# Rotary embedding on one core: the first batch is stored by two DMAs (2 and 30 KB rows) instead of three (2, 14 and 16 KB rows)

## The chip, the cores and the metric

One core of a Trainium2 chip. The metric is the time of one execution on the device in microseconds (us), the median of several runs.

## What is computed

```python
def reference(x, cos, sin):          # x: (8, 2048, 8, 64), cos and sin: (2048, 32), float32
    x1 = x[..., : x.shape[-1] // 2]
    x2 = x[..., x.shape[-1] // 2 :]
    cos = cos[None, :, None, :]
    sin = sin[None, :, None, :]
    out1 = x1 * cos - x2 * sin
    out2 = x1 * sin + x2 * cos
    return np.concatenate([out1, out2], axis=-1)
```

x is 32 MB and is read once; the output has the same size and is written once.

## The kernel before

**Tiles.** Each of the 8 batches is one tile `xt` of 128 partitions by 8192 float32 elements: partition q holds 16 consecutive positions of the sequence (`R = 16`), each of 8 heads by 64 elements, `HD = 512` elements or 2 KB. A row of a tile is thus 32 KB, and a batch is 4 MB. `UNIT` is 4 HD. Five buffers (`NBUF`) hold the tiles; the result is written over x in place, and the tile is stored from there.

**Loads.** All loads are issued from SP's queue (line 67). Batch 0 is loaded in three DMAs (8, 8 and 16 KB rows), every other batch in one DMA with 32 KB rows. The loads of batches 0 to 4 are issued at the start. The load of batch b + 5 is issued after the work of batch b, and waits until batch b's store has freed the buffer.

**Compute.** A batch is worked on in pieces, `pieces(b)`: batch 0 in pieces of 2, 2, 4, 4 and 4 HD, the last one in 4, 4, 4, 2 and 2, the others in four of 4. For a piece of kind A, GpSimd (POOL) multiplies by sin and by -sin (two instructions, line 122), VectorE (DVE) multiplies by cos (line 129), and then adds the two products into `xt` (line 136). Five pieces are of kind B or C, in which TensorE adds the two products with identity matrices and ScalarE (ACT) copies the sum into `xt` (lines 143 to 145 and 160 to 165); in kind C the sin product is DVE's as well (line 148). These are the first pieces of batches 1 to 5.

**Stores.** A batch is stored in the shares that `shares(b)` lists. A share is issued as soon as the pieces that cover it are done (line 74), from ACT's queue, for the last batch from SP's. A store on ACT's queue is issued in ACT's program order, between its copies.

**Order.** The order of the instructions is that of the program (`keep`). The loads and the last batch's stores are in one DMA queue (q1 in the profile), the other stores and the load of sin in another (q10). Both are worked on by the same 16 DMA engines; a DMA over 128 partitions is split into 128 rows, 8 on each engine.

Of the kernel before, what the change touches and what calls it, by code (L numbers as in the profile page):

```python
# [10 lines left out]
def kernel(  # L11
# [15 lines left out]
    HD = H * D  # L27
    R = S // P
    ROW = R * HD
    UNIT = 4 * HD  # L30
# [145 lines left out]

    def shares(b):
        if b == 0:
            return [HD, 7 * HD, 2 * UNIT]
        if b == last:  # L180
            return [2 * UNIT, UNIT, UNIT]
        return [ROW]

    for b in range(B):
        done = 0
        outs = list(spans(shares(b)))
        for lo, n in spans(pieces(b)):
            rotate(b, lo, n)
            done = lo + n
            while outs and sum(outs[0]) <= done:  # L190
                store(b, *outs.pop(0))
        if b + NBUF <= last:
            load(b + NBUF)
# [30 lines left out]
```

## Time and profile before

| what | value |
|---|---|
| median of 3 runs | 163.42 us (163.29 to 163.53) |
| span of the profiled execution, first to last instruction | 161.6 us |
| median less span | 1.8 us |
| DVE busy | 140.1 us (87%) |
| POOL busy | 138.9 us (86%) |
| PE busy | 47.1 us (29%) |
| ACT busy | 12.8 us (8%) |
| read from memory and written to it | 34.08 MB and 33.55 MB, 419 GB/s over the span |

The execution that was profiled is known by its span alone; what lies around the span is taken as the 1.8 us between the span and the median of the runs.

How to read it. Times are from the start of the span. An engine's busy time counts instructions only, no waits. "L122" is line 122 of the kernel. The DMA row of the page is the busy share of the 16 DMA engines in 40 equal slices of the span, in tenths, where 9 stands for 90% or more. The queue table gives for each queue the packets, the megabytes, and the time that its packets took as a share of 16 engines' span. The chain is followed back from the last instruction to what released each step. A timeline line gives start, duration, engine, line, operation, and in brackets how long the engine had been idle before it and what ended that. `ACTq` and `SPq` are the issues of DMAs. The DMA table gives the time from the issue of a DMA to its landing; 4096 KB loads took 40.3 us at the median, most of which is waiting in the queue. The trace also has a record of each DMA packet, with queue, bytes, start and duration.

### The profile page before, as it was taken

The numbers are of one execution on the slowest core, as the hardware profiler recorded it, in microseconds if no ns is written. First come the engines' busy times: TensorE is split into PE (matmuls) and PEld (weight loads), VectorE is DVE, ScalarE is ACT, GpSimd is POOL, SyncE is SP. The second block draws the span as 40 slices with busy tenths as digits, with TensorE's granted clock in tenths as the row PEclk, the third lists the DMA queues.
The fourth block names the chain that finished last, engine by engine and source line by source line (L and its number), as shares of the span: only waits on it lengthen the run. The fifth ranks groups of instructions, "written<-read, shape, count | busy, mean of one in ns | idle before, by whom it ended". The sixth has DMA issues, their size and how long they took to land.

```text
span 161.6 us, 460 instructions
## 1 busy us (share of the span) xinstructions
PE 47.1 (29%) x80; PEld 17.8 (11%) x80; DVE 140.1 (87%) x66; ACT 12.8 (8%) x14; POOL 138.9 (86%) x70
## 2 busy tenths in 40 slices
PE   0000000597209750977039813972000000000000
PEld 0000000143004210322023302330000000000000
DVE  0297999999999999999999999699969999899920
ACT  3300000002200220022000120022000000000000
POOL 1399999999999999976999989997899979999500
PEclk9999999999965997599858995699555555555555
DMA  5999999999999999999999999999999999999995
GB/s 157 419 462 413 424 469 403 394 457 457 410 402 450 442 470 389 454 454 389 470 438 389 471 432 389 462 446 398 446 448 406 430 462 406 430 462 397 414 408 225
DMA packets 3458, 67.65 MB, mean 419 GB/s; under 512 B 384, under 2 KB 384, under 8 KB 768
## 3 DMA queue, kind: packets, MB, share of 16 engines
q1 hardware_dynamic: 2016, 38.01, 55.3%
q10 hardware_dynamic: 1440, 29.62, 42.9%
q14 instruction: 2, 0.02, 0.0%
HBM read 34.08 MB, written 33.55 MB: 419 GB/s over the span
## 4 chain that ended last, share of the span: by engine, by line
DVE 53%; DMA 29%; POOL 9%; issue 5%; DVEq 0%; SPq 0%; POOLq 0%
DVE t L129 28%; DMA xt<-in_x_dram 25%; DVE xt L136 22%; POOL t L122 9%; DMA sin_sb<-in_sin_dram 4%; DVE t L148 3%; DVEq L136 0%; SPq L67 0%; POOLq L122 0%
## 5 line engine op out<-in xcount | busy, mean ns | idle before, releaser
L122 POOL TENSOR_TENSOR t<-xt,sin_sb 128x1024 f32<-128x1024 f32 (+1 forms) x32 | 70.5, 2202 | 12.1 <-DMA xt<-in_x_dram 6.7
L129 DVE TENSOR_TENSOR t<-xt,cos_ps 128x2048 f32<-128x2048 f32 (+1 forms) x34 | 73.4, 2166 | 0.8
L122 POOL TENSOR_TENSOR t<-xt,nsin 128x1024 f32<-128x1024 f32 (+1 forms) x32 | 70.5, 2202 | 0.0
L136 DVE TENSOR_TENSOR xt<-t,t 128x2048 f32<-128x2048 f32 (+1 forms) x29 | 62.2, 2144 | 6.7 <-POOL t L122 4.1
L143 PE MATMUL o<-t,eye 128*128 128x512 f32 x24 | 15.9, 749 | 24.4 <-DVE t L129 21.0
L160 PE MATMUL o<-t,eye 128*128 128x512 f32 x16 | 11.2, 789 | 38.3 <-DVE t L129 36.1
L144 PE MATMUL o<-t,eye 128*128 128x512 f32 x24 | 14.7, 698 | 0.0
L145 ACT COPY xt<-o 128x1024 f32<-128x1024 f32 x6 | 6.1, 1012 | 45.7 <-PE o L144 45.7
L143 PEld LDWEIGHTS o<-t,eye 128*128 128x128 f32 x24 | 5.3, 247 | 33.6 <-issue 27.7
L160 PEld LDWEIGHTS o<-t,eye 128*128 128x128 f32 x16 | 3.7, 256 | 43.8 <-POOL t L122 30.2
L165 ACT COPY xt<-o 128x1024 f32<-128x1024 f32 x4 | 4.0, 1012 | 47.3 <-PE o L161 47.3
L93 DVE COPY cos_ps<-cos_sb 128x512 f32<-128x512 f32 x1 | 0.7, 694 | 7.0 <-DMA cos_sb<-in_cos_dram 7.0
L144 PEld LDWEIGHTS o<-t,eye 128*128 128x128 f32 x24 | 5.4, 227 | 7.4 <-issue 7.4
L161 PE MATMUL o<-t,neye 128*128 128x512 f32 x8 | 6.2, 863 | 0.2 <-DVE t L148 0.2
L148 DVE TENSOR_TENSOR t<-xt,sin_ps 128x2048 f32<-128x2048 f32 x2 | 4.6, 2280 | 0.0
L161 PE MATMUL o<-t,eye 128*128 128x512 f32 x8 | 4.1, 592 | 0.0
L161 PEld LDWEIGHTS o<-t,neye 128*128 128x128 f32 x8 | 1.8, 260 | 4.7 <-issue 3.0
L161 PEld LDWEIGHTS o<-t,eye 128*128 128x128 f32 x8 | 1.5, 190 | 1.9 <-issue 1.9
L90 ACT ACT_TABLE_LOAD x1 | 1.3, 1283 | 1.2 <-PEq L208 1.2
L90 ACT ACTIVATE nsin<-sin_sb 128x512 f32<-128x512 f32 x1 | 0.6, 630 | 4.1 <-DMA sin_sb<-in_sin_dram 4.1
L91 ACT COPY sin_ps<-sin_sb 128x512 f32<-128x512 f32 x1 | 0.6, 579 | 0.0
L80 POOL MEMSET eye<- 128x128 f32 x1 | 0.2, 205 | 0.3 <-POOLq L208 0.3
(6 smaller groups left out, 1.0 us busy)
## 6 DMA issues: line engine op xcount, KB each, us to landing
xt<-in_x_dram SPq DMA_DIRECT2D x7, 4096.0 KB, 40.3
out_dram<-xt ACTq DMA_DIRECT2D x6, 4096.0 KB, 28.3
xt<-in_x_dram SPq DMA_DIRECT2D x2, 1024.0 KB, 6.7
xt<-in_x_dram SPq DMA_DIRECT2D x1, 2048.0 KB, 12.4
out_dram<-xt ACTq DMA_DIRECT2D x1, 2048.0 KB, 25.9
out_dram<-xt SPq DMA_DIRECT2D x1, 2048.0 KB, 11.1
out_dram<-xt SPq DMA_DIRECT2D x2, 1024.0 KB, 7.5
out_dram<-xt ACTq DMA_DIRECT2D x1, 1792.0 KB, 20.8
```

The source lines that it names most:

```text
L90: keep(nc.scalar.mul(nsin, sin_sb, -1.0))
L93: keep(nc.vector.tensor_copy(cos_ps, cos_sb))
L122: nc.gpsimd.tensor_mul(out=t2u[:, :, u, :].rearrange("p (r h) d -> p r h d", h=H), in0=xu[:, :, 1 - u, :].rearrange("p (r h) d -> p r h d" ...
L129: nc.vector.tensor_mul(out=t1.rearrange("p (r k d) -> p r k d", r=nr, d=Dh), in0=xk, in1=rep(cos_ps[:, r0 : r0 + nr, :], 2 * H),)
L136: keep(nc.vector.tensor_add(out=xt, in0=t1, in1=t2))
L143: nc.tensor.matmul(oc, eye, t1[:, cs], start=True, stop=False)
L144: nc.tensor.matmul(oc, eye, t2[:, cs], start=False, stop=True)
L145: keep(nc.scalar.copy(xt[:, 2 * j * C : 2 * (j + 1) * C], o))
L148: nc.vector.tensor_mul(out=t2.rearrange("p (r k d) -> p r k d", r=nr, d=Dh), in0=xk, in1=rep(sin_ps[:, r0 : r0 + nr, :], 2 * H),)
L160: nc.tensor.matmul(oc, eye, t1u[:, gs, u, :], start=True, stop=False)
L161: nc.tensor.matmul(oc, eye if u else neye, t2u[:, gs, 1 - u, :], start=False, stop=True)
L165: nc.scalar.copy(xu[:, :, u, :], o.rearrange("p (g d) -> p g d", d=Dh))
```

## The change

`shares(0)` has two entries instead of three. The first store of batch 0 (1 HD per partition, 2 KB rows) stays. The second and the third (7 HD, issued when the third piece, which ends at 8 HD, is done; and 8 HD, issued when the batch is done) become one of 15 HD, 30 KB rows, which is issued when the batch is done. The instructions of the other engines and their order stay as they were; on ACT one DMA issue is gone.

```diff
     def shares(b):
         if b == 0:
-            return [HD, 7 * HD, 2 * UNIT]
+            return [HD, 15 * HD]
         if b == last:
             return [2 * UNIT, UNIT, UNIT]
         return [ROW]
```

## The prediction

> **What bounds the kernel now.** I read the page's DMA row and queue table first, then the chain, then the DMA table cut to two windows, then the timeline at single instructions.
>
> ```profile
> DVE  0297999999999999999999999699969999899920
> DMA  5999999999999999999999999999999999999995
> q1 hardware_dynamic: 2016, 38.01, 55.3%
> q10 hardware_dynamic: 1440, 29.62, 42.9%
> DVE 53%; DMA 29%; POOL 9%; issue 5%; DVEq 0%; SPq 0%; POOLq 0%
> ```
>
> The 16 DMA engines are busy in every slice between the first and the last: 55.3% + 42.9% = 98.2% of 161.6 us, 158.7 us, which is all the time between the first packet (1.74 us) and the last (160.38 us). So the transfers fill the span. q1 carries SP's loads and the last batch's stores, q10 carries ACT's stores.
>
> The chain names DMA for 29% because of four waits on line 122, each for the load of a new batch (timeline), and the last of them starts the end of the chain (chain in order of time):
>
> ```profile
> 74.11 2.35 POOL L122 TENSOR_TENSOR t<-xt,sin_sb 128x1024 f32<-128x1024 f32 x1 [2.29 <-DMA xt<-in_x_dram]
> 93.61 2.34 POOL L122 TENSOR_TENSOR t<-xt,sin_sb 128x1024 f32<-128x1024 f32 x1 [1.10 <-DMA xt<-in_x_dram]
> 113.71 2.34 POOL L122 TENSOR_TENSOR t<-xt,sin_sb 128x1024 f32<-128x1024 f32 x1 [1.69 <-DMA xt<-in_x_dram]
> 133.08 2.33 POOL L122 TENSOR_TENSOR t<-xt,sin_sb 128x1024 f32<-128x1024 f32 x1 [1.09 <-DMA xt<-in_x_dram]
> ```
>
> ```profile
> 92.59 40.36 DMA xt<-in_x_dram
> ```
>
> Batches 4, 5, 6 and 7 are all waited for. When the loads come later, POOL, then DVE, then the last store come later, unless something absorbs it. At the end stand two things almost level. The compute ends at 154.65 and its last store is issued at 154.67. The engines, still working on the store before it, start this one's rows at 156.97 to 157.94. So a later end of the compute is first absorbed by this queue.
>
> What decides how fast the loads go is how the two queues share an engine. The DMA table, cut to 24 to 53 us, and then to 55 to 110 us:
>
> ```profile
> q1 hardware_dynamic: 298, 8.55, 69.0%
> q10 hardware_dynamic: 307, 4.15, 33.4%
> ```
>
> ```profile
> q1 hardware_dynamic: 405, 12.22, 51.5%
> q10 hardware_dynamic: 395, 11.73, 49.6%
> ```
>
> In both, each queue sends about as many packets as the other. The packet records show why: on each engine one packet of one queue follows one of the other, and a packet is one row (8 rows of each transfer per engine), plus a 4-byte packet that ends the transfer and takes a turn too. So short rows get a small share of the time. A 32 KB row takes 1.213 us, a 16 KB row 0.611, a 14 KB row 0.535. While batch 0 is stored in short rows, the loads have two thirds of the engines; beside 32 KB stores they have half.
>
> **The change, part by part.**
>
> *One DMA fewer on ACT.* A DMA issue takes 0.34 us in ACT's sequencer. The one at 18.43 goes; ACT's next copy runs at 36.64, so this gives 0. The wait for the last piece, at 27.88, is the one that the third store had: no new wait, and nothing new is queued behind it.
>
> *Bytes and packets.* Bytes stay. Eight rows of 30 KB replace eight of 14 KB and eight of 16 KB on each engine. Between the 16 KB row (0.611) and the 32 KB row (1.213) a 30 KB row is 1.138, against 0.535 + 0.611 = 1.146; with one ending packet of 9 ns fewer that is 8 x 0.008 + 0.009, some 0.07 us less. The Trainium skill ("DMA: Bandwidth & Descriptors", section "Anatomy of one DMA", measured there for the GpSimd path) gives a DMA a fixed cost of about 2.0 us; by it the merge would gain, as an estimate, 2 us and give 161.4. The rows above show the engines at work without a gap through these transfers, so I take 0.07.
>
> *The moved store.* Rows 2 to 16 of batch 0's share are issued when its last piece is done:
>
> ```profile
> 18.43 0.34 ACTq L74 DMA_DIRECT2D out_dram<-xt  x1
> ...
> 27.88 0.34 ACTq L74 DMA_DIRECT2D out_dram<-xt  x1
> ```
>
> Before, the 14 KB rows were queued at 18.43 behind the 2 KB rows and started as those ended, at 24.2. Now q10 is empty from 24.2 until the store of 27.88 reaches the engines. Two stores of before met a busy engine in this way: the first 2 KB store (issued 10.38, first rows at 13.83 to 15.06) and the first store of batch 7 (issued 144.77, first rows at 148.20 to 150.07). That is 3.4 to 5.3 us, so the 30 KB rows start between 31.3 and 33.2, and until then loads run alone for 7 to 9 us: 6 to 7 rows per engine (7.1/1.213 = 5.9).
>
> Now count turns from 24.2 to the landing of batch 4. The load queue has three loads, 27 turns. Before, 27 store turns stood beside them: 8 of 14 KB, 8 of 16 KB, 8 of 32 KB (batch 1) and 3 ends, in all 8 x (0.535 + 0.611 + 1.213) = 18.9 us. Now n load rows pass alone and 27 - n turns have a store turn beside them: 9 for the 30 KB store, 9 for batch 1, and 9 - n rows of 32 KB of batch 2. That is 8 x (1.138 + 1.213) + (9 - n) x 1.213 = 18.8 + (9 - n) x 1.213. With n = 6 it is 3.6 us later on the engines where batch 4's load ended early before (ten, at 72.2 to 72.6). Six others were one turn later (73.4 to 73.55) and lose one turn less, 2.4 us. A landing needs all 16 engines, so it moves from 73.55 to about 76: **2.4 us later with n = 6, 1.2 with n = 7, 3.6 with n = 5**. I take 6, since the engine with the fewest rows is the last to finish.
>
> In short: the store of batch 0 overtakes. It ends some 4 us sooner, the following stores too, and the loads pay by two rows. Batch 2 lands earlier (loads alone) and its wait of 0.34 us on POOL at 39.54 goes. Batch 3 lands at 54.5 (issued 7.01, 47.5 to landing), is used at 62.45, and can bear it. Both are worth 0. From batch 4 on both queues are always full and the delay stays. The load of batch 5 waits on line 67 for batch 0's store (issued 53.81); it is issued sooner, but stands in the queue behind batch 4's load: 0.
>
> *What the delay does to the compute.* Batch 4's POOL work starts at 76.5 instead of 74.11. DVE was behind POOL there: its add at 85.49 needs a product that ended at 83.25 and now ends at 85.65, 0.2 late. Batch 5 arrives at 96.0; the add that waited 1.22 us for POOL at 102.85 is now at 105.25: all 2.4 us are on the path. Batches 6 and 7 the same (113.71 to 116.1, 133.08 to 135.5). The compute ends at 157.05, the last store is issued at 157.07.
>
> *What the end absorbs.* The engines finish the store before it at the same time as before, 156.97 to 157.94, and now stand idle. With an empty queue the nearest row is the first load: issued 0.73, first rows at 1.74 to 2.19, 1.0 to 1.5 us. So rows start at 158.1 to 158.5, last 8 x 0.306 = 2.45 us, and the landing follows 0.4 later (before: last packet 160.38, SP sees it at 160.77). That makes 160.9 to 161.4 against 160.77, a loss of 0.15 to 0.65 us; a store may take up to 1.7 to start by the spread of the two rows above, 0.85. I take 0.6, and the 0.07 gained cannot reach the end since the queue is empty. Span 161.6 + 0.6 = 162.2. The median, 163.42, stands 1.8 us above the span, so **164.0**.
>
> **The rule that bears on it.** The packet records show one row for one row. The same page of the Trainium skill (section on queues, rings and completion order) says that an engine drains a packet of some 9 to 17 descriptors from one queue before it turns to the next. By it a whole transfer's 8 rows would pass in one turn, the size of a row would matter little and my delay would vanish: 163.4. The trace disagrees, and I go by the trace.
>
> **Rivals.**
> - *Absorbed.* All engines let 7 rows pass alone: loads 1.2 us later, last store issued at about 155.9, rows ready at 157.4, the engines busy until 156.97 to 157.94 anyway. 163.4. For it: the later half of the 3.4 to 5.3 us. Against it: one early engine is enough.
> - *Three rows.* The store arrives before 30.3 us on one engine: loads 3.6 us later, last store at 158.3, 1.2 us more than forecast, 165.2. Against it: no row shows less than 3.4 us.
> - *Faster, by a level finish.* The last engine ends at 160.38, the earliest at 159.42, their middle is near 159.85. A store queue with fewer, equal turns could level the engines, worth up to 0.5 us, with the 0.07 above 162.9. It decides only while the last store is bound by the engines and not by the compute, that is for a delay below some 0.8 us.
> - *No effect at all*, because the 30 KB rows are cut into smaller packets: then shares stay as with short rows and the loads gain. The 32 KB stores are not cut in the records, so I give it little, and count it with the absorbed case.
>
> **How the numbers follow.** Two rows: 0.50; of this about a quarter falls within 0.2% (0.33 us, about what a measurement of this kernel can tell). Three rows: 0.12. Absorbed: 0.26. Faster: 0.12. So slower 0.38 + 0.12 + 0.05 from the upper part of absorbed = 0.55; same 0.12 + 0.19 = 0.31; faster 0.12 + 0.02 = 0.14. The range reaches from absorbed with some levelling, 163.2, to three rows, 165.2. The forecast's own range is 163.5 to 164.3.
>
> **What would show it.** Right: q10 empty from about 24.2 to 31.3; batch 0's store landing some 4 us before 53.78; POOL's four waits about 76.5, 96.0, 116.1 and 135.5; the last store issued near 157.1, and the engines idle for about half a microsecond before it. Wrong: waits that move by 1.2 or 3.6 (n), waits that stay (arbitration is not by rows), or a last store that is late without the span being longer.

## The result, and the profile after

The changed kernel takes 163.66 us (median of 22 runs, 163.48 to 164.22), the kernel before 163.47 us beside it (22 runs, 163.22 to 163.91). The ratio is 1.0016, with a 95% interval of 1.0008 to 1.0023: slower by 0.2 us, where 0.6 was forecast. The execution whose profile is shown first took 164.22 us, the longest of the 22; two more profiles of the same kernel, of 163.98 and 163.66 us, come in the experiments, and the last of them took as long as the median. One execution of all that follow, the profiled one of the kernel meant to hold its store back by 10 us, took 173.89 us, and neither it nor its profile is used.

The page of the changed kernel, DVE and DMA in 40 slices and the queues:

```profile
span 162.4 us, 458 instructions
...
DVE  0198999999999999999997999379979999899970
DMA  5999999999999999999999999999999999999976
...
q1 hardware_dynamic: 2016, 38.01, 55.4%
q10 hardware_dynamic: 1296, 29.62, 42.3%
```

The DMA engines are still busy in each slice, with one difference: 7 and 6 in the last two slices where 9 and 5 stood. In DVE's row seven slices differ, most by one or two tenths; a 3 stands where a 6 stood near 102 us, in batch 5, and a 7 for a 2 in the last slice but one, where the compute now ends later. The number of q10's packets fell by 144, 128 rows and 16 endings.

The DMA table of the changed kernel, cut to 24 to 31 us:

```profile
q1 hardware_dynamic: 96, 2.92, 97.6%
q10 hardware_dynamic: 11, 0.01, 0.4%
```

Here is the gap in the store queue: the loads have the engines to themselves, where in the kernel before the stores had a third of them (34.1% in the same window). The store that ends it, in the timeline, and the four waits on line 122:

```profile
28.34 0.34 ACTq L74 DMA_DIRECT2D out_dram<-xt  x1
...
77.60 2.32 POOL L122 TENSOR_TENSOR t<-xt,sin_sb 128x1024 f32<-128x1024 f32 x1 [5.31 <-DMA xt<-in_x_dram]
...
97.19 2.32 POOL L122 TENSOR_TENSOR t<-xt,sin_sb 128x1024 f32<-128x1024 f32 x1 [1.18 <-DMA xt<-in_x_dram]
...
116.68 2.34 POOL L122 TENSOR_TENSOR t<-xt,sin_sb 128x1024 f32<-128x1024 f32 x1 [1.10 <-DMA xt<-in_x_dram]
...
136.11 2.32 POOL L122 TENSOR_TENSOR t<-xt,sin_sb 128x1024 f32<-128x1024 f32 x1 [1.14 <-DMA xt<-in_x_dram]
...
157.70 0.33 SPq L74 DMA_DIRECT2D out_dram<-xt  x1
```

POOL's wait for batch 4 is 5.31 us instead of 2.29. Against the kernel before the four instructions start 3.5, 3.6, 3.0 and 3.0 us later, and the last store is issued 3.0 us later, 157.70 for 154.67. The time rose by far less. Where the rest went is seen in the busy shares of two windows (DVE is the third of the columns with an x, DMA the last column but one), first of the kernel before, with the issue of its last store, then of the changed one:

```profile
154.67 0.33 SPq L74 DMA_DIRECT2D out_dram<-xt  x1
...
156.00:158.00 2.00, 0.00 (x0) 0.00 (x0) 0.00 (x0) 0.00 (x0) 0.00 (x0) 0.50 1.03 434
158.00:160.00 2.00, 0.00 (x0) 0.00 (x0) 0.00 (x0) 0.00 (x0) 0.00 (x0) 0.50 0.82 344
```

```profile
156.00:158.00 2.00, 0.00 (x0) 0.00 (x0) 1.57 (x2) 0.00 (x0) 0.00 (x0) 0.50 0.69 291
158.00:160.00 2.00, 0.00 (x0) 0.00 (x0) 0.00 (x0) 0.00 (x0) 0.00 (x0) 0.50 0.81 336
```

Before, the compute is over by 156 us and the engines are full: the last store waits for them, its first rows start 2.3 to 3.3 us after its issue, and it lands 6.1 us after it (154.67 + 6.1 = 160.8). After, DVE still works there and the engines run dry: the store finds them free, its first rows start 0.8 to 1.0 us after its issue, and it lands 3.8 us after it (157.70 + 3.8 = 161.5). Of 3.0 us, 2.3 are absorbed by the queue that is no longer there.

### The profile page after: what moved, and what is told of

It reads as the page before. It is cut to its first block, busy times and chain, and to the rows that moved or that the text cites. A ratio compares the mean times of both kernels' runs of the same rounds, so it can differ in the third digit from the quotient of the medians.

```text
span 162.4 us, 458 instructions
## 1 busy us (share of the span) xinstructions
PE 48.0 (30%) x80; PEld 18.0 (11%) x80; DVE 140.1 (86%) x66; ACT 12.8 (8%) x14; POOL 139.0 (86%) x70
## 4 chain that ended last, share of the span: by engine, by line
DMA 49%; DVE 37%; POOL 9%; issue 2%; DVEq 0%; SPq 0%; ACTq 0%; POOLq 0%
DMA xt<-in_x_dram 27%; DVE t L129 18%; DMA out_dram<-xt 18%; DVE xt L136 17%; POOL t L122 9%; DMA sin_sb<-in_sin_dram 4%; DVE t L148 1%; DVEq L136 0%; SPq L67 0%; ACTq L74 0%; POOLq L122 0%
## 5 line engine op out<-in xcount | busy, mean ns | idle before, releaser
L143 PE MATMUL o<-t,eye 128*128 128x512 f32 x24 | 16.0, 756 | 24.5 <-DVE t L129 21.0
L160 PE MATMUL o<-t,eye 128*128 128x512 f32 x16 | 11.7, 825 | 38.5 <-DVE t L129 36.3
L144 PE MATMUL o<-t,eye 128*128 128x512 f32 x24 | 14.9, 709 | 0.0
L161 PE MATMUL o<-t,eye 128*128 128x512 f32 x8 | 4.1, 592 | 0.0
## 6 DMA issues: line engine op xcount, KB each, us to landing
out_dram<-xt ACTq DMA_DIRECT2D x1, 3840.0 KB, 24.8
```

What stands on the lines that cost most here:

```text
L143: nc.tensor.matmul(oc, eye, t1[:, cs], start=True, stop=False)
L144: nc.tensor.matmul(oc, eye, t2[:, cs], start=False, stop=True)
L160: nc.tensor.matmul(oc, eye, t1u[:, gs, u, :], start=True, stop=False)
L161: nc.tensor.matmul(oc, eye if u else neye, t2u[:, gs, 1 - u, :], start=False, stop=True)
```

## The experiments

Each ran beside the kernel before, whose median was 163.37 to 163.48 us; ratios are to it. Two theories were set against each other. *Turns*: two queues share an engine row by row, and the change lets store rows overtake load rows. *Lateness*: the store costs because its bytes are queued later. A third, a fixed cost per DMA, would show as a gain of each merge.

### The 14 KB store issued late, first try

```diff
-            while outs and sum(outs[0]) <= done:
+            while outs and sum(outs[0]) <= done and (b or lo == 0 or done == ROW):
```

> The kernel before, with its three stores of batch 0, but the 14 KB store is issued at the end of the batch together with the 16 KB one: as late as the changed kernel's, with short rows. Theory of turns (two DMA queues take an engine row by row, and what counts is the number of store rows that stand beside the loads): loads run alone for 6 to 7 rows, and then stand beside 16 short rows, so batch 4 lands some 7 us earlier than before, POOL does not wait for batches 4 to 7, the compute ends near 151, and the time is bound by the full DMA engines, 163.4 (within 0.1% of before). Rival, lateness (the store's bytes were queued 9.4 us later, and that is what cost): at least as slow as the changed kernel, 163.7 or more.

The edit moved nothing. ACT has no instruction between the two stores, and the 14 KB store waits for its own pieces alone, so it was still issued at 18.54. It measured 163.49 us (ratio 1.0004, 0.9994 to 1.0015), and is a repeat of the kernel before: it decides nothing between the theories, and says how well two such medians agree. Its profile has one thing of use. Batch 4's first product started at 73.10, a microsecond earlier than in the first profile of the kernel before. A third kernel that is the same up to its last batch (the one before with its last store halved, below) has it at 74.77: a start moves by 1.7 us from one execution to the next.

### The same, held in earnest

```diff
+            if b == 0 and done == ROW:
+                keep(nc.scalar.copy(late, xts[0][:, ROW - 8 :]))
```

(with the condition of the first try; `late` is a tile of 8 columns that nothing reads)

> The kernel before, with its 14 KB store held to the end of batch 0 by a copy of 8 elements of the last piece on ACT, so that the 14 and the 16 KB store are both issued near 28.4: as late as the changed kernel's, with short rows. Turns: loads run alone for 6 to 7 rows and then stand beside 16 short rows, so batch 4 lands some 6 us earlier than before, POOL waits for no load after batch 3, and the compute ends earlier than before, 152; the end is then that of the engines, 163.4, plus what the start of a store beside a running load stretches (0.2 to 0.5). Lateness (a store that is queued later costs by itself): 163.7 or more, with the engines' last packet late though the compute is early.

163.49 us, ratio 1.0004 (0.9994 to 1.0015). ACT's issues and the waits of POOL:

```profile
27.97 0.82 ACTq L75 DMA_DIRECT2D out_dram<-xt  x2
```

```profile
POOL t L123 <- DMA sin_sb<-in_sin_dram: 5.4, 1, 5.4
POOL t L123 <- DVE xt L137: 2.7, 2, 2.2
```

Both stores are as late as the changed kernel's. There is no line of POOL waiting for `xt`: all loads after the start come in time. The last store is issued at 152.26, 2.4 us earlier than before, and lands 8.6 us later, at 160.9. So short rows, as late, give the loads so much that no load is waited for; and an early end of the compute is worth nothing, since the engines' work sets the end. Lateness alone, at this moment, costs nothing that can be seen here. The pair, this kernel and the changed one, has its stores equally late and differs in the rows: POOL's waits for loads are 8.7 us in all with 30 KB rows (the first profile of the changed kernel) and none with 14 and 16 KB.

### One store, and two halves

```diff
-            return [HD, 7 * HD, 2 * UNIT]
+            return [ROW]
```

> Batch 0 in one store of 32 KB rows, issued at the end of the batch. Turns: no store row stands beside the loads from 13.9 to 31.5, then all of them are long; against the changed kernel nine more load turns pass alone minus the nine of the 2 KB store, which cost next to nothing, and the loads of batches 4 to 7 come 1 to 2.4 us later than in the changed kernel, the last store is issued at 158 to 160, 164.6 to 165.4. Rival, a fixed cost for each DMA: one DMA fewer again, so faster than the changed kernel by what the first merge gained. Rival, lateness: only 256 KB more are late, as the changed kernel, 163.7.

163.57 us, ratio 1.0017 (1.0001 to 1.0034). The waits end at 75.98, 95.54, 115.17 and 134.52, earlier than in the changed kernel and not later; the last store is issued at 156.12. The expectation was miscounted. Up to the landing of batch 4, the engine that lands last has 18 store rows of 32 KB beside its loads, 21.8 us, and in the changed kernel 8 of 2 KB (0.084 us each), 8 of 30 KB and 11 of 32 KB, 23.1 us. Counted so, turns give 1.3 us less; measured it is 0.9 to 1.7 less. In the time no gain by the merge is seen beyond the noise (163.57, and 163.66 for the changed kernel), which speaks against the fixed cost.

```diff
-            return [HD, 7 * HD, 2 * UNIT]
+            return [2 * UNIT, 2 * UNIT]
```

> Batch 0 in two stores of 16 KB rows: issued when 8 HD are done (18.4) and at the end of the batch (27.9). Turns: the first store starts at 21.9 to 23.7, loads run alone for 7 rows from 13.9 where the 2 KB rows stood beside them, then 18 short turns; loads land about 2.4 us later than before, like the changed kernel, 163.6 to 164.0. Lateness: 256 KB come 8 us later and the rest as before, 163.4. Fixed cost: like the changed kernel, since it has one DMA fewer than before too.

163.62 us, ratio 1.0013 (1.0003 to 1.0024). The waits end at 76.04, 95.40, 114.77 and 134.14, 1.1 to 1.9 us later than before, and 1.1 us or more later than in any of the three profiles that start like the kernel before; the last store is issued at 155.73. Its rows are short and only 256 KB of it are later than before; what it has in common with the changed kernel is a time in which no store row stands beside the loads. Turns expect the sign. The size expected, 2.4 us, was too large: counted on the engine that lands last, 16 rows of 16 KB and 10 of 32 KB stand for 8 of 2, 8 of 14, 8 of 16 and 9 of 32 KB, which is 1.1 us more.

### The last store halved, in the changed kernel and in the one before

```diff
-            return [2 * UNIT, UNIT, UNIT]
+            return [2 * UNIT, UNIT, 2 * HD, 2 * HD]
```

> The changed kernel, with the last 1 MB store cut in two of 512 KB (shares of the last batch 2 UNIT, UNIT, 2 HD, 2 HD). If the changed kernel's end waits for the compute (the engines stood idle 0.4 to 1.7 us before its last store), the halves shorten what runs after the compute by 8 x 0.15 = 1.2 us: 0.3 to 0.8 us faster than the changed kernel where the engines idle, 163.1 to 163.4. If the engines' own work sets the end, nothing is gained, 163.6. Rival, a fixed cost of a DMA: slower than the changed kernel.

> The kernel before, with the last 1 MB store cut in two of 512 KB. In the kernel before no engine idled ahead of the last store, so nothing is gained: 163.4, within 0.2%. If the compute set its end too, up to 1.2 us faster, 162.3. Fixed cost of a DMA: slower, 163.8 or more.

On the changed kernel: 163.53 us, ratio 1.0009 (0.9995 to 1.0024). On the kernel before: 163.42 us, ratio 1.0004 (0.9993 to 1.0016). The second is as expected: nothing is gained where the engines set the end. The first gains less than expected, 0.1 us against the change's 163.66, and the intervals overlap, so the time shows no gain. Its profile agrees with the reading. The last store is issued at 157.21, no earlier than in the changed kernel, yet the engines are not dry ahead of it:

```profile
156.00:158.00 2.00, 0.00 (x0) 0.00 (x0) 1.18 (x1) 0.00 (x0) 0.00 (x0) 0.50 0.96 401
```

0.96 for 0.69: half of the data is handed over while the engines still work, and their own end, near 160.6, is back as the limit.

### The changed kernel with its store held back

```diff
+        if b == 1 and lo == 0:            # 2 us: issued at 30.10
+            keep(nc.scalar.copy(late, t1[:, 0:8]))
+            store(0, HD, 15 * HD)
...
+            if b == 1:                    # 4 us: issued at 32.27
+                keep(nc.scalar.copy(late, t2[:, 0:8]))
+                store(0, HD, 15 * HD)
...
+                if b == 1 and u == 0:     # meant as 10 us: after ACT's first copy of batch 1
+                    store(0, HD, 15 * HD)
```

(The comments are not in the code. In all three the condition of the first try, here `and (b or lo == 0)`, keeps the 30 KB store from its old place.)

> The changed kernel, with the 30 KB store held back by another 4.5 us: a copy of 8 elements of batch 1's sine product on ACT stands before it, so it is issued near 32.5. Turns: loads run alone for 10 to 11 rows instead of 6 to 7, which more than makes up for the long rows; batch 4 lands 1 to 2.5 us earlier than before, the compute ends earlier than before, the engines bind, 163.4. Lateness: later is worse, more than the changed kernel, 164.0 or above.

> The changed kernel, with the 30 KB store held back by a copy of 8 elements of batch 1's cosine product on ACT, issued near 30.4, half as far as the store held to 32.5, which measured 165.5. Turns: loads run alone for 8 to 9 rows, batch 4 lands near 74, as before, the compute ends as before, 163.4 to 163.7. Lateness: between the changed kernel and the one held to 32.5, near 164.6. Third theory, the phase between the load and the store of a batch on an engine decides how much load packets are stretched: not in order of the delay, and read from the number and the length of the stretched packets.

> The changed kernel, with the 30 KB store put between the two ACT copies of batch 1's first piece, so that it is issued near 37.7, 10 us later than in the changed kernel. Held back by 2 and by 4.2 us it measured 164.3 and 165.5. Lateness of a store with long rows: worse in order, 167 or more. Stretch (load packets beside the first rows of a new store take longer, and how much depends on where on an engine the store's end stands to the load's end): not in order; the loads land earlier than in the kernel before by some 6 us or more, the compute ends early, the engines set the end, and the time is 163.4 plus the mean stretch and the spread over the engines, between 163.5 and 165.5.

Held by 4 us: 165.50 us, ratio 1.0117 (1.0097 to 1.0138). By 2 us: 164.31, ratio 1.0056 (1.0040 to 1.0073). By 10 us, as it was meant: 163.53 over nine executions, ratio 1.0004 (0.9993 to 1.0015).

The store held by 2 us was expected at 163.4 to 163.7 by turns and near 164.6 by lateness; 164.31 is nearer to lateness. Its profile, of the fastest of its eight executions (163.82), has batch 4 at 74.94 and the last store issued at 154.8, much as before.

At 4 us turns are right on the loads and wrong on the time. The waits of POOL and the last store:

```profile
72.39 2.33 POOL L123 TENSOR_TENSOR t<-xt,sin_sb 128x1024 f32<-128x1024 f32 x1 [0.58 <-DMA xt<-in_x_dram]
...
132.62 2.32 POOL L123 TENSOR_TENSOR t<-xt,sin_sb 128x1024 f32<-128x1024 f32 x1 [1.65 <-DMA xt<-in_x_dram]
...
154.21 0.33 SPq L75 DMA_DIRECT2D out_dram<-xt  x1
```

Batch 4 is there 1.7 us earlier than before, as expected, and the last store is issued 0.5 us earlier; but it lands 8.6 us later, at 162.8, two microseconds later than before. The loss is in the engines. None idles for more than 0.3 us in all after 25 us, and yet the last of them ends at 162.5 us (before: 160.4) and the first at 159.8. The packet records show load packets that are stretched: 32 KB rows that take 1.3 to 2.9 us instead of 1.213. Added up over packets of all kinds that are over 3% too long, it is 25.5 us on 16 engines, 1.6 us for one, against 7.6 us, 0.5 for one, in the kernel before; and it is uneven, from 0.8 to some 3 us. Of the 25.5 us, 11.3 fall between 30 and 40 us. The store held by 2 us has 17.5 us of it, nearly all between 30 and 35 us, where the first store rows meet the running loads.

So a second effect, in no step of the prediction, is at work here, and it does not grow with the delay throughout (163.66, 164.31, 165.50, 163.53 in the order of the delay). It rises up to 4 us, as lateness says; of these four only the last, whose delay no profile here shows, speaks against lateness, beside the short rows held to 28.

### Short rows held to the same moment

```diff
+            if b == 1:
+                keep(nc.scalar.copy(late, t2[:, 0:8]))
+                store(0, HD, 7 * HD)
+                store(0, 8 * HD, 8 * HD)
```

> The kernel before, with its 14 and 16 KB stores both held to 32.6 by the copy of 8 elements on ACT that held the 30 KB store to that time (165.5). Lateness as such: 165.5 again. Stretch: the phase between store and load differs with 18 store turns instead of 9; little stretch after the first rows, 163.4 to 163.8.

164.91 us, ratio 1.0080 (1.0056 to 1.0105): much slower than the same short rows at 28, and nearer to lateness than to my expectation. The compute is early (the last store is issued at 152.21), but that store lands 9.9 us later, at 162.1: again the engines. (The condition is that of the held 30 KB store.) Stretched packets add up to 25.5 us, 6.6 of them between 30 and 45 us and 16.8 between 65 and 80. In this kernel there is a suspect for a part of it, which no run tested by itself: the load queue runs empty. The DMA table from 60.5 to 64.5 us:

```profile
q10 hardware_dynamic: 84, 1.62, 94.3%
q1 hardware_dynamic: 16, 0.00, 0.2%
```

Batch 4 is loaded, batch 5 waits for batch 0's store to free the buffer, and the loads start again at 68.8 beside running stores: 6.2 us of the stretch fall there, between 65 and 70. The other 10.5, between 75 and 80, come as batch 1's store ends. In the 30 KB kernel held to that moment the load queue was never empty; apart from the 11.3 us at the first store rows, its stretches come mostly at the seams between transfers (71 to 76, 93 to 96, 112 to 116 us). What makes a seam costly, and why the kernel held by 10 us shows nothing of it in its times, stays open.

### The changed kernel, again and a third time

> The changed kernel once more, for a second profile: 163.66, and a profile nearer to that median than the first (164.22) shows a smaller delay of the loads: batch 4 waited for until 75.5 to 76.5 instead of 77.6, the last store issued at 156 to 157 instead of 157.7. If the time of a run goes with its stretch instead, the waits are as in the first profile and the engines' ends differ.

> The changed kernel a third time, one look, to see how the waits of batches 4 to 7 and the idle time of the engines ahead of the last store go with the time of the run: with a theory of turns, each 1.2 us of delay of the last store beyond the first 1 to 1.5 us shows in the time.

Again: 163.93 us, ratio 1.0021 (1.0005 to 1.0038), with a profiled execution of 163.98. Third: one run, 163.66, its profile:

```profile
77.21 2.32 POOL L122 TENSOR_TENSOR t<-xt,sin_sb 128x1024 f32<-128x1024 f32 x1 [5.34 <-DMA xt<-in_x_dram]
96.65 2.32 POOL L122 TENSOR_TENSOR t<-xt,sin_sb 128x1024 f32<-128x1024 f32 x1 [1.04 <-DMA xt<-in_x_dram]
116.09 2.32 POOL L122 TENSOR_TENSOR t<-xt,sin_sb 128x1024 f32<-128x1024 f32 x1 [1.07 <-DMA xt<-in_x_dram]
135.53 2.34 POOL L122 TENSOR_TENSOR t<-xt,sin_sb 128x1024 f32<-128x1024 f32 x1 [1.16 <-DMA xt<-in_x_dram]
...
157.13 0.33 SPq L74 DMA_DIRECT2D out_dram<-xt  x1
```

The last store lands 3.9 us later, at 161.0; in the other two profiles it is issued at 157.22 and 157.70 and lands at 161.3 and 161.5. The times go with the landing: 163.66, 163.98 and 164.22. With the issue they go only from end to end, 0.57 us for 0.56; the middle profile has its issue 0.09 later than the third and its time 0.32. In all three most engines idle ahead of the last store's rows, by up to 1.0 to 1.6 us: this is the end that waits for the compute. My expectation of the second profile, a batch 4 at 75.5 to 76.5, was too early; it came at 77.51. The four profiles that start like the changed kernel have batch 4 at 76.84 to 77.60, the three that start like the kernel before at 73.10 to 74.77: later by 2.1 us at the least.

The rows that pass alone can be counted in the packet records of the three. (The records do not name the engine; a packet is put on the engine where another ends as it starts.) It is 7 or 8 on most engines, 6 on one engine in the first and in the second profile, and 6 on four in the third. In all three batch 4's load ends at 73.7 to 75.3 on the engines with 7 or 8 rows, and at 76.4 to 77.1 on those with 6: the landing is set by the few.

## Why the prediction was right or wrong

The range held the time and the direction is right; the forecast, 164.0, was 0.3 us too high. The second series of the changed kernel, 163.93 beside 163.48, is 0.45 us slower and not 0.2, so an agreement to a tenth of a microsecond is not to be leaned on. Step by step:

- *The gap and its length: right for the engine that decides, too short for others.* The earliest 30 KB row starts 3.9 us after the issue (32.2 for 28.34), between 3.4 and 5.3; but in the first profile the engines' first rows start as late as 35.3, 6.9 us after it, seven of them past 5.3. Of the three profiles only the third has them all in the range (31.6 to 33.2, issued at 27.93). The number of rows alone, 6 on the engine that decides, was right, and so was the reason given, that a landing needs all 16.
- *The delay of the loads: right in kind, too small.* Batch 4 came 3.1 to 3.5 us later and not 2.4. The term that I left at nothing is the stretch of the load packets as the first store rows reach them: batch 2's 128 rows took 1.305 us in the mean, in the kernel before 1.244, which is 128 x 0.061 = 7.8 us over 16 engines, 0.5 for one. On the engine that lands last the store rows add the 2.4 us of the sum (8 of 30 KB and 11 of 32 KB for 8 of 14, 8 of 16 and 9 of 32 KB); its stretched packets add about 0.8, and its load rows had begun 0.5 later (14.57 for 14.04), which is within the 1.7 us by which a start moves.
- *Batch 0's store lands earlier: too large.* 28.34 + 24.8 = 53.1 in the first profile, 53.4 in the second and 51.1 in the third, 0.4 to 2.7 us sooner than 53.78 and not 4. The 4 counted from the earliest row (31.3 + 18.8 = 50.1); the rows start one to two microseconds later than I took, they stand beside stretched load rows, and the store ends with its last engine.
- *Through POOL and DVE to the end: right in its numbers, in part by luck.* I expected 96.0, 116.1, 135.5 and an issue at 157.07; the typical profile has 96.65, 116.09, 135.53 and 157.13. The delay was 0.5 to 0.6 us larger at batch 4 than at the last store: the kernel before lost about that much between batches 5 and 6 (113.71 - 93.61 = 20.1 us, 19.4 in the typical profile). That about cancels what the stretch added, and was no step of mine.
- *What the end absorbs: mis-sized, and this is the error of the forecast.* I took a loss of 0.6 us, which is 4.3 us from the issue to the landing, out of a range that began at 3.85. It measured 3.8 to 4.1: on an engine that stands idle rows start 0.8 to 1.0 us after the issue. 157.13 + 3.9 = 161.0 against 160.8 is 0.2 us, the difference of the medians, 163.66 - 163.47. The engines idled 0.6 us in the mean ahead of it in the third profile, near the half microsecond predicted, and 0.4 and 1.0 in the second and the first.
- *The rule on arbitration, weighed in the prediction:* by it batch 4 would have come as early as before; it came 3.1 to 3.5 us later, and the packet records of every run here show one row of one queue and one of the other in turn. The pair of late stores does not decide this point: by the rule, too, two short transfers would take two turns and the merged one a single turn.
- *A reading of the chain: wrong, with no weight in the sum.* The 29% of DMA are not the four waits, which are 6.2 us together: 25% is one load, batch 7's, with its 40.36 us from issue to landing, and 4% the load of sin.
- *Rivals.* Absorbed: the queue at the end did absorb most, though the loads were three microseconds late and not one. A level finish: the engines did end level in the changed kernel, at 161.1 to 161.2, but level with the last store of the compute. Three rows: the delay came near that case's 3.6 us, but no engine had fewer than 6 rows, and the price was not paid at the end.

None of these kernels beats the kernel before. Its engines are busy from 1.7 to 160.4 us, and what the loads gain or lose in between is worth nothing until the compute's last store comes later than they run dry. The exception is the stretch, which lengthens the engines' own work.

## What to carry to other kernels

Where two DMA queues share the engines row by row, the length of a row is a share of the bandwidth: merging the stores of one stage into longer rows takes time from the loads beside it. And a late load is not yet a late kernel: follow it to the last store, and compare that store's issue with the moment at which the engines run out of other work. An early end of the compute is worth nothing for the same reason.

## What the runs showed of the hardware

On each engine a row of one queue and a row of the other pass in turn, so a queue's share goes with the length of its rows: 69.0% for 32 KB load rows beside rows of 14 and 16 KB, 51.5% beside 32 KB. Where a store reaches the engines beside running loads, load packets around it are stretched: 7 to 17 us over 16 engines, 0.4 to 1.0 us for one, in the profiles with a gap in the store queue, and 5 to 11 us in the three profiles of kernels that start like the one before. The two ranges overlap, so that a gap by itself costs more is not shown. Packets at the seam between two transfers can be stretched too, unevenly over the engines; in the kernel where this was seen, the 30 KB store held by 4 us, the time rose by 2 us (163.4 to 165.5) with the compute early and the engines never idle for long. What causes the stretch stays open. On a free engine the first row of a store starts 0.8 to 1.0 us after the issue, and 3.4 to 7.4 us after it where 32 KB rows of the other queue go on.
